# Low parts of split weights from an accumulating transfer, in the planned mixers of a four-layer network

## The chip, the cores and the metric

One core of a Trainium2 chip runs the whole program. The metric is device microseconds of one execution, the median of several runs; less is better.

## The reference

Four layers work on 256 tokens of width 1024, in float32. Each layer is a half-step SwiGLU block, a mixer, and a second half-step SwiGLU block, with root-mean-square norms before and behind each. The mixers are mLSTM (layers 0 and 3), RWKV-7 (layer 1) and retention (layer 2).

```python
for layer in range(DEPTH):
    g = norm_g[layer]
    h = swiglu_ffn(rms_norm(x, g[0]), ffn_w_gu[layer, 0], ffn_w_down[layer, 0])
    x = x + HALF_STEP * rms_norm(h, g[1])
    h = rms_norm(x, g[2])
    kind, j = layer % N_MIXERS, layer // N_MIXERS
    h = mlstm_mixer(...) if kind == 0 else rwkv7_mixer(...) if kind == 1 else retention_mixer(...)
    x = x + rms_norm(h, g[3])
    h = swiglu_ffn(rms_norm(x, g[4]), ffn_w_gu[layer, 1], ffn_w_down[layer, 1])
    x = x + HALF_STEP * rms_norm(h, g[5])
```

mLSTM projects the tokens, convolves q and k, builds input and forget gates, and for each of four heads sums the decayed past: `num = s @ v + inter * (q @ C)`, divided by its denominator, normed by head, gated, and projected back. RWKV-7 has small-rank branches for its decay, its rate and its gate, and a state update for each of 16 heads. For this change only one thing counts: all of it is matrix products with weights of 345 MB in float32, beside the mixers' own small products.

## The kernel before

**Weights.** They come as 345 units of 128 x 2048 float32, 1 MB each. A matmul on float32 weights is made of three on a rounded format (fp32r): every unit is split into a high part, `hi` = the weights rounded, and a low part, `lo` = weights minus `hi`, and `mm3` issues `hi` x high part of the activations, `lo` x high part, `hi` x low part (lines 334 to 336 with the weights standing in the array, 338 to 340 with the weights moving). So nothing of a unit can start until its `hi` is written, and little until its `lo` is.

Four steps bring a unit: `dma()` (L110) puts its load on SyncE's queue into one of `NRAW` = 3 raw buffers; `prep_hi` (L127) lets ScalarE copy, with rounding, from raw to `hi`; `prep_lo` (L135) subtracts `hi` from raw, on VectorE, or on GpSimd if it is handed that engine; and the unit is marked ready. `hi` and `lo` have `NHI` = 5 buffers each. In the FFN blocks and in retention the order of the work is written by hand and a unit is split in two halves of 1024 columns, the subtraction on VectorE. In the two mLSTM layers and in RWKV it is split in quarters of 512 columns.

**The planner.** The bodies of mLSTM and RWKV are written as chains (Python generators): `dense` for the projections, `conv`, `gates`, `attend`, `heads`, `solve`, `finish` and so on, and two `preps` chains that split the weights. Each chain names the engine and the cost in ns of its next piece, or the marks it waits for. `Plan.run` simulates the engines with these costs when the program is built, and takes the piece with the earliest start plus a weight of its chain from the table `PUT_OFF`; VectorE ("ve") and GpSimd ("po") share one resource "port" in it, so that only one of them works at a time there. What it decides is the order of instructions on each engine and nothing else: on the chip every engine takes its own list in that order, and waits at each instruction for what it reads. TensorE can't go past a matmul whose `lo` isn't there.

Of the two `preps` chains one hands its quarters to VectorE (600 ns), the other to GpSimd (1200 ns). They share the same unit: whichever comes first takes the next quarter.

The places that matter are these. In mLSTM, units 36 to 48 in layer 0 (207 to 297 us) and 299 to 311 in layer 3 (1875 to 1985); L925 to L951 make the gates' block of products for a head, L977 and L981 scale it, L993 and L997 are a head's product with its values, L1046 its transposes, L842 the evictions of the projected values, L860 to L871 the convolution. In RWKV, units 115 to 132 (672 to 945 us): L1346 to L1392 form the mixed inputs, L1440 the small-rank products, L1797 to L1881 the inverse for each head pair with the products A16 (L1809), L2020 to L2113 the norm and the last projection, after which L270 to L298 end the layer.

Of the kernel before, what the change touches and what calls it, by code (L numbers as in the profile page):

```python
# [11 lines left out]
F32 = mybir.dt.float32  # L12
# [16 lines left out]
NRAW = 3  # L29
# [5 lines left out]
class Net:  # L35
# [97 lines left out]
    def prep_lo(s, o, src, unit, e=None):  # L133

        (e or s.nc.vector).tensor_tensor(out=o[1], in0=src, in1=o[0].bitcast(F32), op=ALU.subtract)  # L135
        j, h, l, w = unit
        s.split_cols[j] = s.split_cols.get(j, 0) + w
        if s.split_cols[j] < 2048:
            return False
        s.ready[j] = h, l  # L140
        s.dma(j + 1 + NRAW - s.held_raw)
        return True

    def prep_part(s, parts=2, e=None):
        s.prep_lo(*s.prep_hi(parts), e)
# [338 lines left out]
class Stage:  # L484
    HOLD = (0, 0)

    def preps(s, e=None, after=()):
# [4 lines left out]
        while True:  # L492
            yield n.room
            if n.part is None:
                later = [m for m in (("free", n.n_prep + 1 - NHI + n.held_hi), ("raw", n.n_prep)) if m in s.plan.marks]
                if later:
                    yield later
            yield "ac", 520.0
            if not n.room():
                continue  # L500
            o, src, unit = n.prep_hi(4)
            yield ("po", 1200.0) if e else ("ve", 600.0)
            if n.prep_lo(o, src, unit, e):
                s.plan.mark("prep", unit[0])

    def need(s, j):

# [220 lines left out]
class Mlstm(Stage):  # L728
# [1 line left out]


    H, DK, DV = 4, 128, 256
    PUT_OFF = dict(conv=325, gates=300, attend=50, evacs=125, prep=375, prep_po=575, dense=150)
    HEAD = [("v", 0), ("o", 0), ("v", 1)]
    N_AHEAD = 0

# [535 lines left out]
class Rwkv(Stage):  # L1272
# [4 lines left out]

    N_AHEAD = 1
    HOLD = (1, 0)
    PUT_OFF = dict(enter0=500, enter1=450, tail=825, small=150, lora1=275, borrows=250, mix1=50, mix0=200, inv0=50,  # L1280
                   inv1=300, finish=250, norm_in=850, preset=575, evacs=650, w=850, a=875, g=775, norms=175, solve0=350,
                   solve1=250, solve2=225, solve3=325, outputs=375, tr0=150, tr1=675, prep=625, prep_po=450, dense=100,
                   out=775, vec0=300, vec1=175, vec2=600, vec3=425, start0=0, start1=850, start2=425, start3=325,
                   right0=300, right1=0, right2=100, right3=900, rmats0=575, rmats1=425, rmats2=250, rmats3=50, dense2=675)
    ALPHA = math.exp(-0.5)

    def __init__(s, n, gi, d):
# [1057 lines left out]
```

## Time and profile before

| | before |
|---|---|
| median of 3 runs | 2175.19 us (2174.14 to 2177.9) |
| the profiled execution | 2175.98 us, span 2174.2 us |
| mean granted TensorE clock | 0.983 |
| TensorE, VectorE, ScalarE, GpSimd busy | 96%, 69%, 51%, 16% |
| read from HBM | 372.89 MB, 172 GB/s over the span |

The profiled execution is 0.8 us above the median. A busy share is of the whole span. In a window's row the granted clock is a share of full speed, and the DMA share that of 16 DMA engines. "A <- B" in the waits says that A stood idle until B released it.

### The profile page before, as it was taken

What the parts mean: (1) busy time and instruction counts of PE and PEld (TensorE: products, weight loads), DVE (VectorE), ACT (ScalarE), POOL (GpSimd) and SP (SyncE); (2) the same over time, 40 slices, a digit from 0 to 9 for tenths busy, and PEclk for the clock granted to TensorE, in tenths of its full rate; (3) what the DMA queues carried; (4) which work ended last, traced back from release to release, by engine and by line L of the source; (5) the groups of instructions that cost most, each with busy time, mean ns of one, the idle gap of its engine ahead of it and who ended that gap; (6) DMA issues with size and microseconds to landing.
All of it is one profiled execution on the core that took longest, in us unless ns stands there. A gap on an engine that the chain in (4) does not pass through costs nothing.

```text
span 2174.2 us, 38941 instructions
## 1 busy us (share of the span) xinstructions
PE 2091.4 (96%) x16136; PEld 1976.0 (91%) x16136; DVE 1492.2 (69%) x2234; ACT 1112.9 (51%) x1804; POOL 356.2 (16%) x615
## 2 busy tenths in 40 slices
PE   8999989999998999879999999999999999998998
PEld 8999879999997988879999999998999999887997
DVE  6766777667666787677677668556766766757765
ACT  5545655445445754345445445444544554655543
POOL 2001421002000466730001003211000100252000
PEclk9999999999999999889999999999999999999999
DMA  7553245555552320136546555554654555234651
GB/s 278 214 201 136 108 171 211 211 191 195 216 192 98 124 76 31 55 145 251 195 156 244 204 194 194 175 175 146 230 204 169 217 211 194 100 117 191 233 205 68
DMA packets 56226, 376.46 MB, mean 173 GB/s; under 512 B 7144, under 2 KB 8808, under 8 KB 11888
## 3 DMA queue, kind: packets, MB, share of 16 engines
q1 hardware_dynamic: 55472, 372.59, 46.9%
q8 instruction: 127, 2.08, 0.4%
q10 hardware_dynamic: 576, 1.38, 0.2%
q14 instruction: 51, 0.42, 0.1%
HBM read 372.89 MB, written 1.05 MB: 172 GB/s over the span
## 4 chain that ended last, share of the span: by engine, by line
PE 82%; DVE 11%; ACT 3%; issue 2%; POOL 1%; DMA 1%; DVEq 0%; SPq 0%; ACTq 0%; POOLq 0%
PE mm L338 14%; PE mm L340 14%; PE mm L339 14%; PE acc L336 7%; PE acc L334 7%; PE acc L335 7%; PE mm L334 4%; PE mm L335 4%; PE mm L336 4%; DVE lo L135 3%; DVE s L864 1%; ACT hi L127 1%; DVE s L270 1%; DVE x L276 1%; PE acc L1440 1%
## 5 line engine op out<-in xcount | busy, mean ns | idle before, releaser
L135 DVE TENSOR_TENSOR lo<-raw,hi 128x1024 fp32r<-128x1024 f32 (+1 forms) x700 | 810.3, 1200 | 188.6 <-ACT hi L127 186.2
L127 ACT ACTIVATE hi<-raw 128x1024 fp32r<-128x1024 f32 (+1 forms) x766 | 697.7, 964 | 116.5 <-issue 57.0
L338 PE MATMUL mm<-xh,hi 128*128 128x256 f32 x2688 | 743.1, 276 | 0.0
L339 PE MATMUL mm<-xl,hi 128*128 128x256 f32 x2688 | 741.3, 276 | 0.0
L340 PE MATMUL mm<-xh,lo 128*128 128x256 f32 x2688 | 741.2, 276 | 0.0
L339 PEld LDWEIGHTS mm<-xl,hi 128*128 128x128 f32 x2688 | 518.0, 193 | 1.7
L338 PEld LDWEIGHTS mm<-xh,hi 128*128 128x128 f32 x2688 | 518.0, 193 | 1.7
L340 PEld LDWEIGHTS mm<-xh,lo 128*128 128x128 f32 x2688 | 518.1, 193 | 0.0
L336 PE MATMUL acc<-hi,s 128*128 128x512 f32 x864 | 331.3, 383 | 7.4 <-DVE s L1067 6.3
L334 PE MATMUL acc<-hi,s 128*128 128x512 f32 x864 | 333.9, 387 | 4.3 <-ACT s L1063 2.3
L335 PE MATMUL acc<-lo,s 128*128 128x512 f32 x864 | 330.0, 382 | 0.0
L571 ACT ACTIVATE s<-s 128x256 f32<-128x256 f32 x152 | 63.6, 419 | 431.9 <-DVE s L569 431.9
L334 PE MATMUL mm<-hi,xh 128*128 128x256 f32 x960 | 268.8, 280 | 5.3 <-ACT xh L1392 5.3
L335 PE MATMUL mm<-lo,xh 128*128 128x256 f32 x960 | 265.4, 276 | 0.9 <-DVE lo L135 0.9
L336 PE MATMUL mm<-hi,xl 128*128 128x256 f32 x960 | 265.2, 276 | 0.0
L336 PEld LDWEIGHTS acc<-hi,s 128*128 128x128 f32 x864 | 164.9, 191 | 34.1 <-DVE s L1067 7.9
L252 POOL TENSOR_SCALAR rr_v<-ssx 128x1 f32<-128x1 f32 x22 | 5.2, 236 | 1148.7 <-ACT junk L307 1148.6
L334 PEld LDWEIGHTS mm<-hi,xh 128*128 128x128 f32 x960 | 185.5, 193 | 6.8 <-ACT xh L1392 5.6
L334 PEld LDWEIGHTS acc<-hi,s 128*128 128x128 f32 x864 | 165.2, 191 | 26.7 <-ACT s L1063 3.4
L335 PEld LDWEIGHTS mm<-lo,xh 128*128 128x128 f32 x960 | 185.4, 193 | 2.5 <-DVE lo L135 1.3
L336 PEld LDWEIGHTS mm<-hi,xl 128*128 128x128 f32 x960 | 185.4, 193 | 0.2 <-DVE xl L1394 0.2
L335 PEld LDWEIGHTS acc<-lo,s 128*128 128x128 f32 x864 | 165.2, 191 | 21.0
(408 smaller groups left out, 2206.5 us busy)
## 6 DMA issues: line engine op xcount, KB each, us to landing
raw<-in_w SPq DMA_DIRECT2D x345, 1024.0 KB, 4.8
s<-in_g_post SPq DMA_DIRECT2D x12, 512.0 KB, 5.9
x<-in_x ACTq DMA_DIRECT2D x2, 512.0 KB, 6.0
s<-in_rw_l SPq DMA_DIRECT2D x4, 256.0 KB, 6.1
s<-in_rw_ln SPq DMA_DIRECT2D x8, 128.0 KB, 4.2
out<-x SPq DMA_DIRECT2D x3, 256.0 KB, 2.1
s<-in_decay SPq DMA_DIRECT2D x1, 512.0 KB, 6.7
s<-in_rw_zmask SPq DMA_DIRECT2D x1, 320.0 KB
```

The lines of the kernel that those rows point to most:

```text
L127: s.nc.scalar.activation(out=o[0], in_=src, func=AF.Copy)
L135: (e or s.nc.vector).tensor_tensor(out=o[1], in0=src, in1=o[0].bitcast(F32), op=ALU.subtract)
L270: nc.vector.tensor_tensor(out=hg[:, h, :], in0=acc[h], in1=g[:, h * 512:h * 512 + 512], op=ALU.mult)
L276: nc.vector.scalar_tensor_tensor(out=s.x[t][:, c], in0=hg[:, h, :], scalar=r, in1=s.x[t][:, c], op0=ALU.mult, op1=ALU.add)
L334: mm(out, ah, wh, start=first, stop=False)
L335: mm(out, ah, wl, start=False, stop=False)
L336: mm(out, al, wh, start=False, stop=last)
L338: mm(out, wh, ah, start=first, stop=False)
L339: mm(out, wh, al, start=False, stop=False)
L340: mm(out, wl, ah, start=False, stop=last)
L571: nc.scalar.activation(out=sg, in_=gn[:, 0, :], func=AF.Silu)
L864: nc.vector.scalar_tensor_tensor(out=c[:, g, :], in0=x[:, g, j:j + T], scalar=s.cw[:, 4 * g + h, j:j + 1], in1=c[:, g, :], op0=ALU.mult, o ...
```

## The change

The GpSimd chain no longer subtracts. It takes a whole unit; ScalarE copies each quarter to `hi` and then writes `lo` = −`hi` (a copy with scale −1.0); when all four quarters stand, GpSimd issues one transfer that reads the unit again from HBM and adds it into `lo`, `lo` = −`hi` + weights. The planner is told 520 ns of ScalarE for each piece and 1500 ns of GpSimd for the issue, and that the unit is ready 4000 ns behind that, with 2700 ns of the DMA resource. Only one unit can be in part in that chain, so either chain waits for the other where it used to share. The weights `PUT_OFF` of both planned mixers are replaced. The diff, where the last table's rows are cut:

```diff
--- before.py
+++ after.py
@@ -141,6 +141,10 @@
         s.dma(j + 1 + NRAW - s.held_raw)
         return True
 
+    def prep_add(s, j, l):
+
+        s.nc.gpsimd.dma_start(out=l, in_=s.w[j], accum_op=ALU.add)
+
     def prep_part(s, parts=2, e=None):
         s.prep_lo(*s.prep_hi(parts), e)
 
@@ -495,13 +499,39 @@
                 later = [m for m in (("free", n.n_prep + 1 - NHI + n.held_hi), ("raw", n.n_prep)) if m in s.plan.marks]
                 if later:
                     yield later
+            if e and n.part is not None:
+                yield lambda: n.part is None
+                continue
             yield "ac", 520.0
-            if not n.room():
+            if not n.room() or e and n.part is not None:
                 continue
             o, src, unit = n.prep_hi(4)
-            yield ("po", 1200.0) if e else ("ve", 600.0)
-            if n.prep_lo(o, src, unit, e):
+            if e:
+
+                j, h, l, w = unit
+                raw = n.part[0]
+                n.part = None
+                n.n_prep = j + 1
+                yield from s.prep_dma(j, raw, h, l)
+                continue
+            yield "ve", 600.0
+            if n.prep_lo(o, src, unit):
                 s.plan.mark("prep", unit[0])
+
+    def prep_dma(s, j, raw, h, l):
+        n = s.n
+        for q in range(4):
+            c = slice(q * 512, q * 512 + 512)
+            if q:
+                yield "ac", 520.0
+                n.nc.scalar.activation(out=h[:, c], in_=raw[:, c], func=AF.Copy)
+            yield "ac", 520.0
+            n.nc.scalar.activation(out=l[:, c], in_=h.bitcast(F32)[:, c], func=AF.Copy, scale=-1.0)
+        yield "po", 1500.0
+        n.prep_add(j, l)
+        n.ready[j] = h, l
+        n.dma(j + 1 + NRAW - n.held_raw)
+        s.plan.load("prep", j)
 
     def need(s, j):
 
@@ -730,7 +760,7 @@
 
 
     H, DK, DV = 4, 128, 256
-    PUT_OFF = dict(conv=325, gates=300, attend=50, evacs=125, prep=375, prep_po=575, dense=150)
+    PUT_OFF = dict(conv=950, gates=750, attend=375, evacs=925, prep=925, prep_po=975, dense=650)
     HEAD = [("v", 0), ("o", 0), ("v", 1)]
     N_AHEAD = 0
 
@@ -1277,11 +1307,12 @@
 
     N_AHEAD = 1
     HOLD = (1, 0)
-    PUT_OFF = dict(enter0=500, enter1=450, tail=825, small=150, lora1=275, borrows=250, mix1=50, mix0=200, inv0=50,
...
+    PUT_OFF = dict(enter0=350, enter1=675, tail=650, small=325, lora1=975, borrows=1000, mix1=525, mix0=650, inv0=450,
...
     ALPHA = math.exp(-0.5)
 
     def __init__(s, n, gi, d):
```

The planner's lists come out otherwise in the three stages, and only there; TensorE has as many instructions as before. Lines 147 to 495 move by 4 in the changed kernel, later ones by 30, and from L1310 on by 31. By the lists, the subtractions of 512 columns on GpSimd go from 66 (18, 30 and 18) to none, those on VectorE from 22 to 28 in each mLSTM and from 42 to 52 in RWKV; ScalarE gets 44 negations, and GpSimd 11 transfers: units 39, 42 and 44; 123, 125, 127, 130 and 132; 302, 305 and 307.

**Layer 0's mLSTM, around unit 44.** In names like `hi44_3023` the number after `hi` is the unit; `s_249` and the like are small tiles. ScalarE before:

```order
L842 ACT_TABLE_LOAD
L842 ACTIVATE s_249_2991<-mm_240_2909,rs0_98 128x256
L842 ACTIVATE s_249_2991<-mm_240_2909,rs1_99 128x256
L1063 ACTIVATE s_251_3001<-mm_250_2996,ml_g_35_407 128x256 x2
L127 ACTIVATE hi44_3023<-raw44_2800 128x512 x3
L868 ACTIVATE s_241_2922<-s_247_2960 128x2x256
L977 ACT_TABLE_LOAD
L977 ACTIVATE s_256_3068<-mm_254_3044,ml_acol_202_2584 128x256
L977 ACTIVATE s_256_3068<-mm_254_3044,ml_acol_202_2584 128x128
```

and now:

```order
L127 ACTIVATE hi45_2892<-raw45_2819 128x512
L529 ACTIVATE lo44_2884<-hi44_2883 128x512
L527 ACTIVATE hi44_2883<-raw44_2761 128x512
L529 ACTIVATE lo44_2884<-hi44_2883 128x512
L527 ACTIVATE hi44_2883<-raw44_2761 128x512
L872 ACTIVATE s_246_3012<-mm_239_2920,rs0_98 128x256
L872 ACTIVATE s_246_3012<-mm_239_2920,rs1_99 128x256
L529 ACTIVATE lo44_2884<-hi44_2883 128x512
L1093 ACTIVATE s_249_3025<-mm_248_3020,ml_g_35_407 128x256 x2
```

Before, unit 44's quarters are copied once, and the evictions of unit 42's product stand ahead of them (L842). Now three negations (L529) stand ahead of those evictions (L872) and the last one behind.

TensorE there, where head 2's product with its values (L993) stood between units 43 and 44 (`s_259` is that of L842), before:

```order
L334 MATMUL mm_253_3010<-hi43_2871,xh_152_2054 128x256
L335 MATMUL mm_253_3010<-lo43_2872,xh_152_2054 128x256
L336 MATMUL mm_253_3010<-hi43_2871,xl_153_2055 128x256
L993 MATMUL mm_260_3097<-s_259_3088,s_257_3069 128x256 x3
L997 MATMUL mm_255_3045<-ones_91,s_257_3069 128x1 x3
L334 MATMUL mm_261_3107<-hi44_3023,xh_152_2054 128x256
L335 MATMUL mm_261_3107<-lo44_3024,xh_152_2054 128x256
```

and now:

```order
L340 MATMUL mm_258_3100<-hi44_2883,xl_153_2055 128x256
L1023 MATMUL mm_260_3136<-s_259_3113,s_257_3092 128x256 x3
L1027 MATMUL mm_255_3069<-ones_91,s_257_3092 128x1 x3
L338 MATMUL mm_258_3100<-hi44_2883,xh_152_2054 128x256
L339 MATMUL mm_258_3100<-lo44_2884,xh_152_2054 128x256
```

That product now comes behind the first 24 matmuls of unit 44, and it is unit 44's `lo` that the transfer makes.

**RWKV's entry.** TensorE before, behind the last matmul of the FFN (L1351 transposes a tile of 128 tokens, `acc` and `mm` are PSUM tiles):

```order
L336 MATMUL acc_493_5659<-hi114_7152,s_595_7084 128x512
L1351 MATMUL mm_629_7359<-ident_90,s_628_7355 128x128 x4
L1351 MATMUL mm_632_7376<-ident_90,s_628_7355 128x128 x4
L334 MATMUL mm_640_7426<-hi115_7251,xh_606_7297 128x256
L335 MATMUL mm_640_7426<-lo115_7252,xh_606_7297 128x256
L336 MATMUL mm_640_7426<-hi115_7251,xl_607_7298 128x256
```

and now:

```order
L340 MATMUL acc_493_5662<-hi114_7155,s_595_7087 128x512
L1382 MATMUL mm_629_7349<-ident_90,s_628_7346 128x128 x4
L1382 MATMUL mm_630_7362<-ident_90,s_628_7346 128x128 x4
L1471 MATMUL acc_639_7430<-s_608_7285,s_620_7330 128x128
L1471 MATMUL acc_639_7430<-s_610_7287,s_624_7334 128x128
```

Where unit 115 followed, the 32 small-rank products (L1440 before, L1471 now) come first, and unit 115 after them.

**RWKV, around unit 125.** GpSimd before:

```order
L135 TENSOR_TENSOR lo124_8210<-raw124_8115,hi124_8209 128x512 x2
L1756 TENSOR_SCALAR s_689_8042<-s_689_8042,rw_par_487_5650,rw_ka1_546_6419 128x256 x2
L135 TENSOR_TENSOR lo125_8271<-raw125_8193,hi125_8270 128x512
L1809 TENSOR_TENSOR q_661_7809<-q_661_7809,ident_90 128x512 x2
L1758 TENSOR_TENSOR s_673_7958<-s_673_7958,s_689_8042 128x512
L1760 TENSOR_TENSOR gx_663_7811<-s_673_7958,s_706_8139 128x512
L135 TENSOR_TENSOR lo125_8271<-raw125_8193,hi125_8270 128x512
L1766 TENSOR_TENSOR s_673_7958<-s_711_8273,s_673_7958 128x512
```

and now:

```order
L1787 TENSOR_SCALAR s_684_8014<-s_684_8014,rw_par_487_5653,rw_ka1_546_6422 128x256 x2
L1789 TENSOR_TENSOR s_672_7912<-s_672_7912,s_684_8014 128x512
L1791 TENSOR_TENSOR gx_663_7835<-s_672_7912,s_705_8123 128x512
L1797 TENSOR_TENSOR s_672_7912<-s_711_8223,s_672_7912 128x512
L1799 TENSOR_TENSOR s_711_8223<-s_711_8223,s_704_8122 128x512
L1840 TENSOR_TENSOR q_661_7833<-q_661_7833,ident_90 128x512
L146 DMA lo125_8299<-in_w 128x2048
L1745 COPY s_728_8410<-ident_90 8x256
L1840 TENSOR_TENSOR q_661_7833<-q_661_7833,ident_90 128x512
```

The four subtractions between go, and the transfer for unit 125 is issued between the two products A16 (L1809 before, L1840 now). In the order of TensorE 24 matmuls of unit 124 and two groups of four head products stand between the first of these products and unit 125.

More of the change, by code (lines that the diff above doesn't have):

```diff
@@ L1279 @@
     HOLD = (1, 0)
-    PUT_OFF = dict(enter0=500, enter1=450, tail=825, small=150, lora1=275, borrows=250, mix1=50, mix0=200, inv0=50,
[L1281 to L1284, printed above, removed]
+    PUT_OFF = dict(enter0=350, enter1=675, tail=650, small=325, lora1=975, borrows=1000, mix1=525, mix0=650, inv0=450,
+                   inv1=400, finish=575, norm_in=800, preset=1175, evacs=450, w=900, a=575, g=800, norms=125, solve0=150,
+                   solve1=325, solve2=350, solve3=600, outputs=675, tr0=1350, tr1=1675, prep=625, prep_po=825, dense=1075,
+                   out=825, vec0=550, vec1=50, vec2=575, vec3=400, start0=1525, start1=925, start2=75, start3=500,
+                   right0=1150, right1=600, right2=750, right3=500, rmats0=500, rmats1=200, rmats2=525, rmats3=750,
+                   dense2=625)
     ALPHA = math.exp(-0.5)
```

## The prediction

> **What bounds the kernel now.** I read the page's span and engine rows first, then the chain that ended last, the costliest groups and the DMA part, then the stretches in which the planner sets the order.
>
> ```profile
> span 2174.2 us, 38941 instructions
> PE 2091.4 (96%) x16136; PEld 1976.0 (91%) x16136; DVE 1492.2 (69%) x2234; ACT 1112.9 (51%) x1804; POOL 356.2 (16%) x615
> q1 hardware_dynamic: 55472, 372.59, 46.9%
> PE 82%; DVE 11%; ACT 3%; issue 2%; POOL 1%; DMA 1%; DVEq 0%; SPq 0%; ACTq 0%; POOLq 0%
> raw<-in_w SPq DMA_DIRECT2D x345, 1024.0 KB, 4.8
> ```
>
> TensorE is busy for 96% of the span and carries 82% of the chain; VectorE carries 11%. The change removes no TensorE instruction, so all it can win are the 2174.2 − 2091.4 = 82.8 us in which TensorE stands, and stretches at a lower clock. The windows say where those lie: first the mLSTM of layer 0, the RWKV layer and the mLSTM of layer 3, then RWKV's inside and its exit into the next FFN. Columns are us, busy time of each engine, granted clock, DMA share, GB/s.
>
> ```profile
> 207.00:297.00 90.00, 82.34 (x602) 76.46 (x601) 60.48 (x117) 54.85 (x110) 37.43 (x76) 0.94 0.36 134
> 672.00:945.00 273.00, 239.96 (x2302) 217.85 (x2301) 205.02 (x413) 152.22 (x361) 142.00 (x179) 0.94 0.23 84
> 1875.00:1965.00 90.00, 81.78 (x607) 76.12 (x606) 60.65 (x117) 54.65 (x111) 37.45 (x76) 0.96 0.38 135
> 752.00:932.00 180.00, 162.92 (x1713) 147.18 (x1712) 133.60 (x262) 87.60 (x216) 127.26 (x164) 0.94 0.18 63
> 932.00:952.00 20.00, 10.36 (x37) 8.23 (x36) 14.97 (x32) 7.38 (x13) 0.00 (x0) 0.66 0.55 209
> ```
>
> TensorE stands 7.7 us in the first mLSTM, 8.2 in the second and 33.0 in RWKV, of which 17.1 lie inside (752 to 932) and 9.6 at the exit. The rest, about 34 us, lies where the order is written by hand and no unit changes hands. So at most about 49 us are in play, and the kernel outside these stretches I count as unchanged. The waits of TensorE, mLSTM 0 first, RWKV behind:
>
> ```profile
> PE acc L993 <- DVE s L981: 2.7, 2, 1.8
> PE mm L993 <- ACT s L842: 1.8, 1, 1.8
> PE mm L1046 <- DVE s L1025: 0.8, 1, 0.8
> ```
> ```profile
> PE mm L292 <- DVE x L276: 8.3, 1, 8.3
> PE mm L334 <- ACT xh L1392: 5.3, 1, 5.3
> PE acc L1879 <- DVE gx L1869: 2.1, 3, 1.0
> ```
>
> Nowhere does TensorE wait for a low part made by GpSimd; it waits for VectorE and ScalarE. GpSimd matters by what it does to VectorE.
>
> **The subtractions on GpSimd go.** There are 66 of them, 18 + 30 + 18, and these are the rows on them and on VectorE's own, the third and fourth from mLSTM 0 and RWKV:
>
> ```profile
> L135 POOL TENSOR_TENSOR lo<-raw,hi x66: 1263/1286/1871, 209.5 to 1961.3; 128x512 fp32r<-128x512 f32 x66
> L135 DVE TENSOR_TENSOR lo<-raw,hi x43: 657/696/2117, 672.4 to 938.0; 128x512 fp32r<-128x512 f32 x39, 128x1024 fp32r<-128x1024 f32 x4
> L135 DVE TENSOR_TENSOR lo<-raw,hi 128x512 fp32r<-128x512 f32 x21 | 19.2, 916 | 1.8 <-ACT hi L127 1.8
> L135 DVE TENSOR_TENSOR lo<-raw,hi 128x512 fp32r<-128x512 f32 x39 | 39.2, 1010 | 11.7 <-ACT hi L127 9.8 <-issue 1.9
> ```
>
> And at the end of RWKV, first with GpSimd's subtraction beside them, then without:
>
> ```profile
> 917.95 1.73 POOL L135 TENSOR_TENSOR lo<-raw,hi 128x512 fp32r<-128x512 f32 x1
> 918.47 1.24 DVE L2079 TENSOR_SCALAR rw_st<-rw_st 128x4 f32<-128x4 f32 x1
> 919.74 0.65 DVE L206 TENSOR_SCALAR nr_y<-rw_st 128x4 int32<-128x4 int32 x1
> 920.74 0.88 DVE L220 TENSOR_TENSOR nr_u<-nr_y 128x4 f32<-128x4 f32 x1
> 923.03 1.13 DVE L240 TENSOR_SCALAR rw_rs<-nr_y 128x4 f32<-128x4 f32 x1
> 924.20 1.45 DVE L2085 TENSOR_TENSOR s<-s,rw_rs 128x256 f32<-128x256 f32 x1
> 927.99 1.75 DVE L135 TENSOR_TENSOR lo<-raw,hi 128x512 fp32r<-128x512 f32 x1
> 930.98 0.17 DVE L2079 TENSOR_SCALAR rw_st<-rw_st 128x4 f32<-128x4 f32 x1
> 931.19 0.17 DVE L206 TENSOR_SCALAR nr_y<-rw_st 128x4 int32<-128x4 int32 x1
> 931.39 0.16 DVE L220 TENSOR_TENSOR nr_u<-nr_y 128x4 f32<-128x4 f32 x1
> 932.97 0.17 DVE L240 TENSOR_SCALAR rw_rs<-nr_y 128x4 f32<-128x4 f32 x1
> 933.17 0.43 DVE L2085 TENSOR_TENSOR s<-s,rw_rs 128x256 f32<-128x256 f32 x1
> ```
>
> One quarter on VectorE takes 0.70 us in the median, but 1.01 in RWKV's mean and 0.92 in mLSTM's. The timeline shows why: the same instruction on four numbers a partition lasts 1.24 us while GpSimd subtracts and 0.17 twelve microseconds later, when it has stopped. VectorE is held while GpSimd subtracts. On quarters alone that is 39 × (1.01 − 0.70) = 12.1 us in RWKV and 21 × (0.92 − 0.70) = 4.6 in an mLSTM.
>
> The Trainium skill, SBUF — State Buffer, section "Who interferes with whom", has a rule for this: an instruction of VectorE with two SBUF inputs comes through the read interface that GpSimd reads by, and one of the two waits. The rows agree for the subtractions and the products; they go beyond it for the four-number TENSOR_SCALAR. By the rule, GpSimd's products, which stay, hold VectorE as well.
>
> At RWKV's exit these six instructions lie in one chain on VectorE, up to the last projection and the FFN's norm, and no matmul is left to cover it: the first waiter is L292, with 8.3 us. The excess is 1.07 + 0.48 + 0.72 + 0.96 + 1.02 + 1.05 = 5.3 us. GpSimd's products at L2062 to L2077 stay, so I take −4 (bounds −5.3 and 0). Inside RWKV, VectorE is relieved of up to 12.1 us but takes over ten quarters (by the order 52 in place of 42): 10 × 0.70 = 7.0, net −5 of its 205. TensorE there stands 17.1 us, in many pieces of at most 1 us or so that VectorE ends, as the L1879 row has them. I take a third of it, −5.7, as a quarter on VectorE shrinks by a third (bounds: −8.5, half, and +4, since every piece is also a place of the new order). In an mLSTM VectorE takes six quarters more, 4.2 us, for the 4.6 won: nothing, at 60.5 busy of 90.
>
> **The negations on ScalarE.** 44 more copies of 512 elements, 12 + 20 + 12, at a third of the first row's time, 0.55 us: 6.6 us in an mLSTM, 11.1 in RWKV.
>
> ```profile
> 238.33 1.66 ACT L127 ACTIVATE hi<-raw 128x512 fp32r<-128x512 f32 x3
> 275.98 0.84 ACT L842 ACTIVATE s<-mm,rs 128x256 f32<-128x256 f32 x2
> ```
>
> ScalarE is busy for 54.9 of 90 and 152.2 of 273 us, so it has 35 and 121 idle; I cost them at nothing but for the place in the queue, counted with the orders below. If that cover is gone, a later copy for the next unit costs 0.6 us each time.
>
> **The adding transfers.** Eleven of 1 MB, three, five and three, issued by GpSimd. The trace has none, so I bound one. Below: the plain load, 4.8 us, plus one GpSimd quarter of 1.3 us for its issue, 6.1. Above: twice the load and that, 10.9. Between them stands a full second pass: q1's 372.59 MB are 355.3 units of 1.05 MB, and their packets take 46.9% of 2174.2 us, 2.87 us a unit, which gives 9.0. I take half of that pass, 7.5, as nearest to the plain row, the one such row there is. Their traffic is no bound: the DMA share is 0.36 and 0.23.
>
> What counts is whether the transfer lands before TensorE asks. TensorE's rows around a gate block:
>
> ```profile
> 249.16 0.28 PE L335 MATMUL mm<-lo,xh 128*128 128x256 f32 x1
> 249.27 0.28 PE L336 MATMUL mm<-hi,xl 128*128 128x256 f32 x1
> 249.38 0.60 PE L1046 MATMUL mm<-ident,s 128*128 128x128 f32 x4
> 251.25 0.36 PE L338 MATMUL mm<-xh,hi 128*128 128x256 f32 x1
> ```
>
> Dense matmuls start 0.11 us apart, and a group of transposes with the gate block L946 to L951 takes 1.9 us, from 249.38 to 251.25. Unit 44: its last negation stands on ScalarE behind the pair L842 that evicts unit 42's product, so it ends 0.84 + 0.55 = 1.4 us after unit 42 does. TensorE still has 48 matmuls of unit 43 (5.3) and one such group with its block (1.9): 7.2 us, so 5.8 are left. At 7.5 the wait is 1.7, at 6.1 0.3, at 10.9 5.1. Counted alike, unit 39 has 12 us left and unit 42 8.6, so they wait only above that. In RWKV unit 125's transfer is issued right behind the first of the two products A16 (L1809), and ahead of the unit TensorE has 24 matmuls of unit 124 (2.7 us) and two groups of four small head products that wait for that A16, some 2.3 with their wait, an estimate by the block above: 5.0 left, 2.5 of wait at 7.5. Units 123, 127, 130 and 132 have 5 to 8 or more: nothing at 7.5.
>
> The Trainium skill, Collectives: The Full Stack, section "Why ReduceScatter is half of AllGather", speaks against this: an add needs two source reads, and its rate was half of a copy's. By it the full second pass would be due, and the sum would be that of rival 1's transfers, 4.5 us higher; no row here shows it.
>
> **The new orders.** mLSTM, by the waits above: unit 39's twelve matmuls no longer stand ahead of head 0's L993, so its 0.9 grows by their 1.4; at head 1 the scaling L977, which feeds L981, is moved ahead of the convolution's activation L868 on ScalarE, and the 1.8 goes; head 1's transposes L1046 get twelve matmuls of unit 43 ahead of them, −0.8; head 2's L993, 1.8 behind L842, comes after 24 of unit 44 and waits no more; head 3's L993 loses part of its cover as unit 45 is taken earlier, +1.1 by half of those 24. The sum is 1.4 − 1.8 − 0.8 − 1.8 + 1.1 = −1.9. With unit 44's +1.7 an mLSTM gives −0.2, both −0.4 (bounds −3.8 and +6.4, unit 44's wait from none to 5.1). RWKV's entry: 32 small-rank products (L1440) now stand ahead of unit 115, and the mixes on ScalarE and VectorE that feed them pace TensorE where it had dense work; L334 waits 5.3 for L1392 there already. Fewer quarters ahead of the norm speak for less, the pacing for more: +2 (bounds −2 and +6).
>
> **The sum.** mLSTM −0.4, exit −4, inside −5.7, entry +2, unit 125 +2.5: −5.6 on the profiled execution's 2175.98, 2170.4. That execution is 0.8 above the median of the three runs, 2175.19; on that base, which the rivals' times use too, it is 2169.6. I say 2170. What a measurement of this kernel can tell from no change is about 0.2%, 4.4 us.
>
> **The rivals.**
> 1. The gains are eaten by late transfers. At the full second pass, 9.0 us, unit 44 and its twin in layer 3 wait 3.2 each and unit 125 4.0: 1.5 × 3 = 4.5 more than in my sum. Unit 42's 8.6 is passed by 0.4, twice, and if the gain inside RWKV is a half of mine the sum is −5.6 + 4.5 + 0.8 + 2.9 = +2.6, 2177.8. For it: VectorE's net relief is only 5 us of 205. Against: the chain's VectorE rows at the exit.
> 2. Slower: an adding transfer takes 10.9 us, the load twice, or more. Then unit 44 and its twin wait 5.1 each and unit 125 5.9, 3 × 3.4 = 10.2 above my sum; units 42 and 305 lack 2.3 each, 123, 127 and 130, with 5 to 8, some 4 each, +16.6; −5.6 + 10.2 + 16.6 = +21.2, 2196.4. It decides from where the sum passes 4.4, at about 9.5 us. For it: nothing in this trace reads two sources. Against: 4.8 us for a plain load while the queues are idle over half the time.
> 3. Slower by the order: RWKV's entry at +6 and inside at +4, with the exit unchanged since GpSimd's products still hold VectorE: −0.4 + 0 + 4 + 6 + 2.5 = +12.1, 2187.3. For it: 17 of RWKV's 33 idle us lie inside and 5 in the row of L1392.
> 4. The change does less than it says, with VectorE held by GpSimd's other work as before: exit and inside at a quarter, −0.4 − 1 − 1.4 + 2 + 2.5 = +1.7, 2176.9, within 0.2%; counted with rival 1.
>
> **How the numbers follow.** The forecast, a gain of over 4.4 us, 0.48; rivals 1 and 4, 0.27; rival 2, 0.15; rival 3, 0.10. Faster is the first, same the second, slower the last two, 0.25. The likeliest case's own range goes from 2155.6 (mLSTM −1.9 twice, exit −5.3, inside −8.5, entry −2, no wait: −19.6) to 2170.8. The whole one reaches from 2157, with a little of that end left out, to 2187, rival 3's value; rival 2's 2196 is left out.
>
> **What would show it.** No L135 on POOL, VectorE quarters near 0.70 us in both mixers, and the L2079 to L2085 chain at RWKV's exit under 3 us where it took 6 would show the relief; L292's wait stays near 8. The time from GpSimd's issue to landing decides rivals 1 and 2: about 7.5 or less is the forecast; above 9 there is a new TensorE wait on a DMA at units 44, 307 and 125. An idle of over 15 us at 672 to 692 would show rival 3. The forecast is wrong above all if TensorE, which runs in its written order, stands behind one late low part while later units are ready.

## The result and the profile after

The changed kernel takes 2209.46 us (median of 4 runs, 2209.06 to 2212.5) where the kernel before, in the runs beside it, takes 2176.18: a ratio of 1.0159 with a 95% interval of 1.0146 to 1.0171, 33 us slower. I had forecast 2170 and a range of 2157 to 2187. Rival 2 is what happened, and it is worse than I had it.

The page after, on the profiled execution (2209.24 us): span, engines, DMA queues, the chain that ended last, and issues to landing.

```profile
span 2207.5 us, 38892 instructions
PE 2099.7 (95%) x16136; PEld 1982.8 (90%) x16136; DVE 1466.0 (66%) x2256; ACT 1141.9 (52%) x1852; POOL 274.8 (12%) x560
q1 hardware_dynamic: 55472, 372.59, 46.3%
q0 software_dynamic: 1584, 11.54, 2.8%
PE 82%; DVE 8%; ACT 5%; DMA 3%; issue 2%; POOL 0%; DVEq 0%; SPq 0%; ACTq 0%
raw<-in_w SPq DMA_DIRECT2D x345, 1024.0 KB, 4.8
lo<-in_w POOLq DMA_DIRECT2D x11, 1024.0 KB, 9.7
```

DMA has 3% of the chain where it had 1%, VectorE 8% where it had 11%. An adding transfer lands 9.7 us behind its issue in the median. The rows of the eleven, of TensorE's waits, and of VectorE's quarters in mLSTM 0 and RWKV:

```profile
DMA to landing us min/median/max: 8.0/9.7/11.4
PE mm L344 <- DMA lo<-in_w: 18.9, 2, 10.0
PE mm L339 <- DMA lo<-in_w: 9.7, 4, 3.6
L135 DVE TENSOR_TENSOR lo<-raw,hi 128x512 fp32r<-128x512 f32 x28 | 18.9, 682 | 1.8 <-ACT hi L127 1.6
L135 DVE TENSOR_TENSOR lo<-raw,hi 128x512 fp32r<-128x512 f32 x51 | 37.9, 752 | 24.4 <-ACT hi L127 24.0
```

TensorE waits 28.6 us for six of the eleven transfers: two in RWKV (L344) and four in the mLSTM layers (L339). In L342 to L344, before L338 to L340, the weights stand in the array, and in L338 to L340, before L334 to L336, they move; where the kernel before is described, the two are the wrong way round. VectorE's relief is there as told: a quarter takes 0.68 us where it took 0.92, and 0.75 where it took 1.01. It doesn't help while TensorE stands.

The two long waits are at units 123 and 125. ScalarE, GpSimd and TensorE around unit 123, from the timeline:

```profile
754.56 0.63 ACT L529 ACTIVATE lo<-hi 128x512 fp32r<-128x512 f32 x1
755.49 0.95 POOL L146 DMA_DIRECT2D lo<-in_w  x1 [1.60 <-ACT lo L529]
765.60 0.55 PE L344 MATMUL mm<-q,lo 128*128 128x256 f32 x1 [10.02 <-DMA lo<-in_w]
765.95 0.42 PE L342 MATMUL mm<-q,hi 128*128 128x256 f32 x1
```

The last negation ends at 755.2, GpSimd, which waited for it, issues at 755.5, and TensorE arrives at 755.6: 765.60 less the 10.02 that it waits. Next to no time lies between the issue and the need. And when it goes on, its matmuls take 0.42 us where 0.28 is usual, and start 0.21 us apart where 0.11 is usual, until 770.2: the granted clock is 0.50 from 760.0 to there.

That is the second cost. The mean granted clock over the span, of before, after and four kernels told below (no11 without the transfers, memset with GpSimd writing zeros, split4, mix), by their views of cores:

```profile
core 0: 2174.2 us, clock 0.983
core 0: 2207.5 us, clock 0.976
core 0: 2170.7 us, clock 0.981
core 0: 2143.6 us, clock 0.989
core 0: 2201.5 us, clock 0.971
core 0: 2167.6 us, clock 0.982
```

The share not granted is (1 − 0.983) × 2174.2 = 37 us before and (1 − 0.976) × 2207.5 = 53 after. Not all of these 16 us are lost time: at unit 123 the clock goes to half at 760.0, and TensorE stands until 765.6 anyway. What the slow clock can have cost shows in TensorE's busy time, 2099.7 us where it was 2091.4 for the same 16136 matmuls: 8.3 of the 33 us. For the other 25 TensorE stands, 107.8 us in all where it stood 82.8.

By stage, from the last start of the SwiGLU activation (L571, L601 after) in the FFN ahead of a mixer to the first in the one behind it, less the same of before, in us; the other kernels are told below. The last column is the timed median less that of before in the same runs:

| kernel | mLSTM 0 | RWKV | mLSTM 3 | whole |
|---|---|---|---|---|
| after | +0.7 | +23.0 | +9.3 | +33.3 |
| no2 | +3.7 | −0.3 | +8.9 | +12.8 |
| no11 | −2.0 | +0.5 | −1.7 | −2.8 |
| plain | −2.0 | +16.8 | −1.5 | +14.5 |
| sub | +1.6 | +9.5 | +2.5 | +9.8 |
| split4 | −0.9 | +27.3 | +0.9 | +24.7 |
| fix10 | −4.6 | +23.4 | −2.4 | +18.0 |
| qadd | −1.8 | +21.8 | +3.1 | +25.0 |
| dveall | +6.1 | +37.0 | +6.8 | +42.4 |
| memset | −13.2 | −5.5 | −11.9 | −29.9 |
| mslong | −9.2 | −5.3 | −11.2 | −27.5 |
| ms22 | −8.8 | −1.6 | −7.6 | −21.6 |
| noneg | −2.1 | +3.7 | −1.5 | −4.9 |
| ne22 | −2.7 | −0.5 | −1.4 | −4.7 |
| mix | −4.6 | +2.2 | −4.0 | −6.7 |

The two mLSTM layers have the same order, and yet after has +0.7 and +9.3: their transfers landed after 9.2, 9.7 and 8.0 us in the first and after 9.6, 11.3 and 9.3 in the second. A stage's number is good to some 3 us: no2, which changes nothing in the mLSTM layers, has +3.7 and +8.9, and noneg and no11, which differ little, have +3.7 and +0.5 in RWKV. The stages are those of one profiled execution, which lies some 4 us above its kernel's median in sub, split4, ms22 and noneg and 8 above in dveall, so they need not add up to the last column.

### The profile page after: what moved, and what is told of

Its sections match the earlier page's. It is cut to its first block, busy times and chain, and to the rows that moved or that the text cites. A ratio compares the mean times of both kernels' runs of the same rounds, so it can differ in the third digit from the quotient of the medians.

```text
span 2207.5 us, 38892 instructions
## 1 busy us (share of the span) xinstructions
PE 2099.7 (95%) x16136; PEld 1982.8 (90%) x16136; DVE 1466.0 (66%) x2256; ACT 1141.9 (52%) x1852; POOL 274.8 (12%) x560
## 4 chain that ended last, share of the span: by engine, by line
PE 82%; DVE 8%; ACT 5%; DMA 3%; issue 2%; POOL 0%; DVEq 0%; SPq 0%; ACTq 0%
PE mm L342 14%; PE mm L344 14%; PE mm L343 14%; PE acc L340 7%; PE acc L338 7%; PE acc L339 7%; PE mm L339 4%; PE mm L338 4%; PE mm L340 4%; DMA lo<-in_w 3%; DVE lo L135 2%; ACT hi L127 2%; DVE s L274 1%; DVE x L280 1%; PE mm L1990 1%
## 5 line engine op out<-in xcount | busy, mean ns | idle before, releaser
L342 PE MATMUL mm<-xh,hi 128*128 128x256 f32 x2688 | 742.5, 276 | 0.0
L344 PE MATMUL mm<-xh,lo 128*128 128x256 f32 x2688 | 740.8, 276 | 0.0
L127 ACT ACTIVATE hi<-raw 128x1024 fp32r<-128x1024 f32 (+1 forms) x733 | 680.3, 978 | 109.0 <-issue 56.5
L342 PEld LDWEIGHTS mm<-xh,hi 128*128 128x128 f32 x2688 | 517.7, 193 | 1.7
L344 PEld LDWEIGHTS mm<-xh,lo 128*128 128x128 f32 x2688 | 517.6, 193 | 0.0
L340 PE MATMUL acc<-hi,s 128*128 128x512 f32 x864 | 331.8, 384 | 9.1 <-DVE s L1097 8.1
L338 PE MATMUL acc<-hi,s 128*128 128x512 f32 x864 | 334.4, 387 | 5.6 <-ACT s L1093 2.6
L339 PE MATMUL acc<-lo,s 128*128 128x512 f32 x864 | 330.5, 383 | 0.0
L601 ACT ACTIVATE s<-s 128x256 f32<-128x256 f32 x152 | 63.6, 418 | 432.7 <-DVE s L599 432.7
L339 PE MATMUL mm<-lo,xh 128*128 128x256 f32 x960 | 267.5, 279 | 9.7 <-DMA lo<-in_w 9.7
L338 PE MATMUL mm<-hi,xh 128*128 128x256 f32 x960 | 270.6, 282 | 0.0
L340 PE MATMUL mm<-hi,xl 128*128 128x256 f32 x960 | 266.8, 278 | 0.0
L339 PEld LDWEIGHTS mm<-lo,xh 128*128 128x128 f32 x960 | 187.2, 195 | 11.7 <-DMA lo<-in_w 6.3
L340 PEld LDWEIGHTS acc<-hi,s 128*128 128x128 f32 x864 | 165.2, 191 | 35.7 <-DVE s L1097 9.8
L338 PEld LDWEIGHTS acc<-hi,s 128*128 128x128 f32 x864 | 165.5, 192 | 28.7 <-ACT s L1093 3.5
L338 PEld LDWEIGHTS mm<-hi,xh 128*128 128x128 f32 x960 | 187.0, 195 | 1.3 <-issue 1.0
L340 PEld LDWEIGHTS mm<-hi,xl 128*128 128x128 f32 x960 | 187.2, 195 | 0.0
L339 PEld LDWEIGHTS acc<-lo,s 128*128 128x128 f32 x864 | 165.6, 192 | 21.1
L599 DVE TENSOR_TENSOR s<-mm,R 128x512 f32<-128x512 f32 x152 | 104.6, 688 | 83.9 <-PE mm L344 83.9
```

Source lines behind the costliest of these rows:

```text
L127: s.nc.scalar.activation(out=o[0], in_=src, func=AF.Copy)
L338: mm(out, ah, wh, start=first, stop=False)
L339: mm(out, ah, wl, start=False, stop=False)
L340: mm(out, al, wh, start=False, stop=last)
L342: mm(out, wh, ah, start=first, stop=False)
L344: mm(out, wl, ah, start=False, stop=last)
```

## The experiments

Each edit is against the changed kernel unless the text says otherwise, and is shortened.

### Is it the transfers, or the new order?

**no2.** The changed kernel without the transfers of units 123 and 125; the rest stands where it stood.

```diff
-        n.prep_add(j, l)
+        j in (123, 125) or n.prep_add(j, l)
```

> The changed kernel without the transfers of units 123 and 125 (their low parts stay the negated high parts, so two units lack their low parts); every other instruction stands where it stood. Theory A, late landing: TensorE's waits of 10.0 and 8.9 us for these two and the two half-clock stretches of 10.24 us behind them go, and little else: 2180 to 2186. Theory B, the new order and the added work of ScalarE are slow by themselves, and TensorE would have stood there anyway for something else: 2200 or more, with another wait in place of the 18.9 us.

Measured: 2188.11 us, 21 less than after, ratio to before 1.0056 (1.0041 to 1.0071). That is 2 us above theory A's range and far from B's. RWKV comes back by 23.3 us, to −0.3. The two waits are 18.9 of these; the other 4 fit the slow stretches, since TensorE is busy 4.9 us less than in after (2094.8 us). What remains slow are the mLSTM layers, +3.7 and +8.9, with four waits of 10.5 us in both.

**no11.** None of the eleven.

```diff
-        n.prep_add(j, l)
+        pass
```

> The changed kernel without any of the eleven adding transfers (eleven units lack their low parts); the order is the same. Theory A: all 28.6 us of waits for these transfers and the half-clock stretches behind them go, 2170 to 2178, so that order, negations and VectorE's relief together come out at about the kernel before, or below it. Theory B: 2190 or more.

Measured: 2172.55 us, ratio 0.9987 (0.9977 to 0.9996). So the transfers cost 36 us (+33.3 against −2.8), and everything else in the change, VectorE's relief, 44 negations and the new orders, comes out at −2.8. Theory A holds. But 2.8 us is little for relief, and I come back to it.

### What makes a transfer late?

**plain.** The same transfers without the addition.

```diff
-        s.nc.gpsimd.dma_start(out=l, in_=s.w[j], accum_op=ALU.add)
+        s.nc.gpsimd.dma_start(out=l, in_=s.w[j].bitcast(F32R))
```

> The changed kernel with eleven plain transfers of the same units by the same queue at the same places, without the addition (eleven units have the whole weights as low parts). If the second source read makes the transfer slow: landing 5 to 7 us after the issue where it is 9.7 with the addition, TensorE's waits at units 123 and 125 about 6 and 5, at 42, 44, 305 and 307 none: 2186 to 2193. If it is GpSimd's queue and its issue: landing still at 9 to 10 us, 2205 to 2210.

Measured: 2189.84 us, ratio 1.0074 (1.0054 to 1.0094): the first case, with waits of 5.8 and 6.2 us at units 123 and 125. Queue, landing and waits:

```profile
q0 software_dynamic: 1584, 11.54, 1.5%
lo<-in_w POOLq DMA_DIRECT2D x11, 1024.0 KB, 6.8
PE mm L344 <- DMA lo<-in_w: 12.0, 2, 6.2
```

The addition takes the DMA engines 2.8% of 2207.5 us for 11 units, 5.6 us each, where the plain copy takes 1.5% of 2187.4, 3.0 us. The time to landing goes from 6.8 to 9.7. So the order of sizes is: 4.8 us for a plain load on SyncE's queue, 2.0 more for the plain copy on GpSimd's, 2.9 more for the addition. The plain copy also writes a tile of the rounded format, which the load doesn't, so the 2.0 need not be the queue's alone. The Trainium skill, Collectives: The Full Stack, section "Why ReduceScatter is half of AllGather", says of a collective's reduce that its add needs two source reads; the two transfers here agree, with 1.9 times the engines' time. And yet plain loses 17 us in RWKV: at units 123 and 125 it lands after 7.4 and 7.7 us, so even a transfer of the 7.5 us of my sum comes too late there.

**sub.** GpSimd's four subtractions at the place of each transfer, so a unit is ready 5.2 us later than there.

```diff
-        n.prep_add(j, l)
+        for each quarter c: n.nc.gpsimd.tensor_tensor(out=l[:, c], in0=raw[:, c], in1=h[:, c], op=subtract)
```

> The changed kernel with GpSimd's four subtractions of 512 columns at the place of each transfer, in the new order; 5.2 us a unit. Theory A: waits at units 123 and 125 of about 5 and 4 us, none at 42, 44, 305 and 307, and VectorE held again as before the change for up to 10 us in each mLSTM and 16 in RWKV, of which a part shows: 2185 to 2200, faster than with the transfers although VectorE loses its relief. Theory B (the order is what is slow): 2205 or more.

Measured: 2185.06 us, ratio 1.0044 (1.0029 to 1.0059): as forecast, but not by the waits forecast. TensorE's waits for GpSimd's low parts are 0.8 us:

```profile
PE mm L344 <- POOL lo L531: 0.8, 3, 0.3
```

A unit's quarters come one by one, where the transfer sets one mark for the whole unit: at unit 123 the four end 1.2 us apart, and TensorE waits 0.2, 0.3 and 0.3 us and goes on with each. So an adding transfer at the same places is 24 us worse than the subtractions it replaces, with all that these do to VectorE.

**split4.** Each transfer in four, each behind its own negation.

```diff
+            n.nc.scalar.activation(out=l[:, c], ..., scale=-1.0); n.nc.gpsimd.dma_start(out=l[:, c], in_=n.w[j][:, c], accum_op=ALU.add)
-        n.prep_add(j, l)
```

> The changed kernel with each adding transfer cut into four of 512 columns, each issued as soon as its own quarter is negated; order of all other work unchanged. If the time is that of moving the bytes twice behind the last negation: the last quarter lands 3 to 6 us after its issue, TensorE's 28.6 us of waits fall to 8 to 15: 2188 to 2198. If it is a fixed delay of such a transfer, or four issues of 0.9 us in a row on GpSimd take it back: waits of 25 us or more, 2203 to 2212.

Measured: 2199.69 us, ratio 1.0115 (1.01 to 1.013), between the two forecasts, and by other means than either.

```profile
lo<-in_w POOLq DMA_DIRECT2D x44, 256.0 KB, 8.3
PE mm L344 <- DMA lo<-in_w: 5.2, 2, 3.0
PE mm L339 <- DMA lo<-in_w: 2.4, 4, 1.7
POOL lo L529 <- ACT lo L529: 50.6, 10, 17.9
```

A quarter takes 8.3 us to land, little less than a unit, but TensorE's waits fall to 7.6 us. The mLSTM layers are back at −0.9 and +0.9. RWKV isn't (+27.3): the issues stand earlier in GpSimd's list and wait there for ScalarE, and GpSimd's products behind them are late, as a wait of TensorE of 3.6 us for L1799 shows that the changed kernel doesn't have. The windows around RWKV, of no11 first and of split4 behind, show how its time comes about (engines in the order TensorE, its weight loads, VectorE, ScalarE, GpSimd; then clock, DMA share, GB/s):

```profile
645.00:980.00 335.00, 302.16 (x2693) 274.96 (x2693) 228.61 (x485) 189.97 (x426) 110.99 (x169) 0.93 0.26 91
646.00:1008.00 362.00, 317.68 (x2698) 288.84 (x2698) 234.53 (x485) 190.36 (x426) 123.92 (x189) 0.89 0.32 99
```

TensorE stands 44.3 us in place of 32.8, 11.5 more, and is busy 317.68 in place of 302.16, 15.5 more, with the same work at a granted clock of 0.89 in place of 0.93: together the 27 us. The larger part is the slow clock.

**fix10.** Why was there no time between issue and need? In `prep_dma` the unit is put into `n.ready` when the transfer is issued, and `need()` asks for the unit's mark only if it isn't in that list. So a chain that asks for a unit after its issue doesn't wait for the mark, 4000 ns or more behind, that `load` sets; its matmuls may be placed right behind the issue, and at units 123 and 125 they were. (The change's description says that the planner holds the unit back for these 4000 ns; it does so only where a chain asked before the issue.) fix10 asks for the mark wherever there is one, and sets it 9.7 us behind the issue.

```diff
-        if j not in n.ready:
+        if j not in n.ready or ("prep", j) in s.plan.marks:
             yield [("prep", j)]
...
-        s.plan.load("prep", j)
+        s.plan.marks["prep", j] = s.plan.end + 9700.0
```

> The changed kernel where the planner waits for the unit's mark before it places its matmuls, and the mark stands 9.7 us after the issue as measured; in the changed kernel the unit counts as ready at its issue, as the list of ready units is filled there and need() then skips the mark. The plan is made anew with the same weights. Theory: the wait comes from matmuls placed as if the transfer took no time; with the true time TensorE's waits for transfers fall from 28.6 to under 6 us, 2172 to 2188. Rival: nothing else can be placed there, so TensorE stands for something else or the unit still comes too soon: 2198 or more.

Measured: 2193.05 us, ratio 1.0077 (1.0062 to 1.0092). The first half of the theory holds, the waits for transfers go from 28.6 to 5.2 us; the time lies between the theory's and the rival's, since RWKV stays at +23.4. These are all of its waits for transfers, and the first of its waits in RWKV:

```profile
PE mm L339 <- DMA lo<-in_w: 2.8, 3, 1.9
PE acc L339 <- DMA lo<-in_w: 1.7, 1, 1.7
PE mm L344 <- DMA lo<-in_w: 0.7, 1, 0.7
...
PE acc L340 <- DVE s L2157: 7.9, 2, 6.9
PE mm L350 <- DVE gx L1782: 7.5, 1, 7.5
PE mm L296 <- DVE x L280: 6.3, 1, 6.3
PE mm L1981 <- DVE s L1977: 6.2, 3, 4.7
```

The delay is turned into waits for VectorE: of these rows after has L296 with 6.1 and L1981 with 2.5, and the other two not at all. My reading is that with the dense matmuls placed later less is left to cover RWKV's chains of small products, and that the weights which order them, being those of the other plan, don't fit; no run shows this. In the mLSTM layers, though, the true landing helps: −4.6 and −2.4.

**qadd.** The old order, with each of GpSimd's 66 quarters negated by ScalarE and added by a transfer of 256 KB at its place.

```diff
+        o[1] of GpSimd's quarters: nc.scalar.activation(out=o[1], in_=o[0], func=Copy, scale=-1.0)
+        nc.gpsimd.dma_start(out=o[1], in_=s.w[j][:, columns], accum_op=ALU.add)
```

> The kernel before in its own order, where each of the 66 quarters that GpSimd subtracted is negated by ScalarE and added by a transfer of 256 KB that GpSimd issues at the same place. VectorE's relief as in memset (2145), plus 66 copies on ScalarE and 66 issues. If a quarter lands some 4 to 5 us behind its issue and TensorE takes it later than that: 2148 to 2162. If it comes late as the units did: waits of TensorE for transfers of 15 us or more with their half-clock stretches, 2180 or more.

Measured: 2201.11 us, ratio 1.012 (1.0103 to 1.0137). The second case: 21.9 us of waits for transfers, fifteen of them, though a quarter lands after 5.3 us.

```profile
PE mm L340 <- DMA lo<-in_w: 17.3, 11, 4.4
PE acc L335 <- DMA lo<-in_w: 3.2, 2, 2.0
PE mm L335 <- DMA lo<-in_w: 1.4, 2, 0.7
```

### What is VectorE's relief worth, and where did it go?

**memset.** The kernel before, in its own order, where GpSimd writes zeros and reads nothing.

```diff
-        (e or s.nc.vector).tensor_tensor(out=o[1], in0=src, in1=o[0].bitcast(F32), op=ALU.subtract)
+        e.memset(o[1], 0.0) if e else s.nc.vector.tensor_tensor(...)
```

> The kernel before, in its own order, with GpSimd writing zeros where it subtracted (66 quarters lack their low parts): GpSimd reads no SBUF there, so VectorE isn't held by it, and nothing else moves. It prices the relief by itself. If my terms of relief (exit -4, inside RWKV -5.7, mLSTM 0) hold and the new order ate them: 2163 to 2168. If TensorE's path has other waits behind those: 2171 to 2176.

Measured: 2145.08 us, ratio 0.9861 (0.9846 to 0.9876): 30 us less, more than twice the larger of the two forecasts. Most of it is in the mLSTM layers, where I had priced the relief at nothing. TensorE's waits in the first mLSTM, of memset first and of no11 behind:

```profile
PE acc L993 <- DVE s L981: 1.5, 2, 0.8
PE acc L334 <- ACT s L1063: 1.1, 2, 0.6
PE acc L947 <- ACT s L929: 0.9, 1, 0.9
PE mm L993 <- ACT s L842: 0.6, 1, 0.6
PE acc L336 <- DVE s L1067: 0.4, 2, 0.2
```
```profile
PE acc L340 <- DVE s L1097: 4.1, 2, 3.9
PE acc L1023 <- DVE s L1011: 3.3, 1, 3.3
PE acc L338 <- ACT s L1093: 1.3, 2, 0.7
```

In memset no wait is over 0.9 us, and the granted clock of this stretch is 0.98 where before has 0.92; over the whole span it is 0.989, 24 us not granted where before lost 37. The longest of the waits that are gone is this one of before:

```profile
PE acc L336 <- DVE s L1067: 3.2, 2, 3.0
```

It ends at 300 us and, in layer 3, at 1969. The windows of the prediction ended at 297 and 1965, so its list of waits lacks it; in no11 it is still there, as L340 and L1097.

**mslong.** memset with two and a half writes for one, so that GpSimd is busy as long as its subtraction was.

```diff
-        e.memset(o[1], 0.0)
+        [e.memset(x, 0.0) for x in (o[1], o[1], o[1][:, :256])]
```

> The kernel memset with two and a half writes in place of one, about 1.3 us of GpSimd for each quarter, as long as its subtraction was, and still no read of SBUF. If it is GpSimd's read that held VectorE: 2145 to 2152. If it is that GpSimd was free sooner, for its own work on the path: 2165 to 2176.

Measured: 2148.35 us, ratio 0.9876 (0.9861 to 0.989), so 27 of the 30 us stay. The engines of memset first and of mslong behind, to be held against VectorE's 1492.2 us and GpSimd's 356.2 in before:

```profile
PE 2079.1 (97%) x16136; PEld 1966.9 (92%) x16136; DVE 1448.7 (68%) x2234; ACT 1111.9 (52%) x1804; POOL 294.3 (14%) x615
PE 2079.0 (97%) x16136; PEld 1966.5 (92%) x16136; DVE 1449.8 (67%) x2234; ACT 1113.0 (52%) x1804; POOL 350.6 (16%) x747
```

With the same 2234 instructions VectorE is busy 43 us less, whether GpSimd writes for 33 us or for 89. It is GpSimd's reading that holds VectorE, not GpSimd's time: the Trainium skill, SBUF — State Buffer, section "Who interferes with whom", says that a two-input instruction of VectorE contends with a GpSimd instruction that reads SBUF and not with one that only writes it, and this pair of runs agrees. One thing stays open: the zeros don't wait for ScalarE's `hi` as the subtractions did, so GpSimd also comes earlier to its own work; no run tells what that gives of the 30 us.

**noneg.** no11's order without the 44 negations too; GpSimd writes zeros in the place of each transfer.

```diff
-            n.nc.scalar.activation(out=l[:, c], in_=h.bitcast(F32)[:, c], func=AF.Copy, scale=-1.0)
-        n.prep_add(j, l)
+        n.nc.gpsimd.memset(l, 0.0)
```

> The changed kernel without the eleven transfers and without the 44 negations (GpSimd writes zeros into the unit where the transfer was issued; eleven units lack their low parts); order of all else as changed. Against no11 (2172.6) it takes away only ScalarE's added work. If the negations are what keeps the relief of 30 us from showing: 2145 to 2158. If it is the new order with VectorE's 22 more quarters: 2167 to 2174.

Measured: 2171.29 us, ratio 0.9977 (0.9965 to 0.9989), against no11's 2172.55: the negations cost nothing that can be told, as predicted.

**ms22 and ne22.** The new plan gives VectorE 22 quarters more. ms22 adds as many to memset's old order, ne22 takes as many (21 by the trace) out of noneg's new one.

```diff
ms22 -        e.memset(o[1], 0.0) if e else subtract on VectorE
ms22 +        e.memset(o[1], 0.0) if e and (count of e) % 3 else subtract on VectorE
ne22 -        subtract on VectorE
ne22 +        nc.gpsimd.memset(o[1], 0.0) if (count of quarters) % 5 == 0 else subtract on VectorE
```

> The kernel memset (old order, GpSimd writing zeros, 2145) with every third of its 66 zeroings done as a subtraction by VectorE at the same place, so 22 more quarters on VectorE, as many as the change adds there; 44 quarters lack their low parts. If VectorE's added quarters (22 x 0.70 = 15 us of its time) eat the relief: 2160 to 2172. If the new order does: 2146 to 2154.

> The mirror of ms22: the kernel noneg (new order, no transfers, no negations, 2171) with every fifth of VectorE's quarters, some 22, zeroed by GpSimd in place of the subtraction; these lack their low parts too. If VectorE's added quarters eat the relief: 2148 to 2158. If the new order does: 2165 to 2172.

Measured: ms22 2154.21 us, ratio 0.9899 (0.9882 to 0.9915); ne22 2171.09, ratio 0.9984 (0.9972 to 0.9996). Both lie with the second case, ms22 at its edge: the added quarters cost 9 us in the old order and nothing that can be told in the new one. With the same quarters on VectorE, no transfer and no negation, the new order (noneg) is 17 us behind the old one (ms22). How the 30 us of relief divide depends on what is taken first: some 9 for VectorE's added share and then 17 for the order, or, from memset to ne22 to noneg, 26 for the order and then nothing for the share. Either way the order is the larger part. I can point at two places of that order in mLSTM, the rows of no11 above: L1023, head 0's product, has lost unit 39's matmuls ahead of it and waits 3.3 us where it waits 0.7 in memset (1.0 in before), and L340 waits 3.9 for L1097 where it waits 0.2 (3.0 in before). For RWKV I have only the sums; which of its many moves cost it stays open.

**dveall.** VectorE makes all low parts, planned anew with the old weights.

```diff
-        chains: prep=preps[0], prep_po=preps[1]
+        chains: prep=preps[0]
```

> The kernel before without GpSimd's chain: VectorE makes every low part, planned anew with the old weights. VectorE takes over 66 quarters at 0.70 us, 46 us in three stages, and is no longer held, about 38 us by the rows of before. If it has the room: 2168 to 2178, as good as with GpSimd's help. If low parts come late (VectorE in RWKV is at 75%): 2182 or more, with waits of TensorE for VectorE's lo.

Measured: 2217.43 us, ratio 1.0188 (1.0171 to 1.0205), the slowest of all. The time is that of the second forecast, but not by its sign: TensorE's waits for VectorE's low parts are 3.4 us in all, and the longest are for other work of VectorE:

```profile
PE mm L2104 <- DVE s L2096: 12.0, 1, 12.0
PE acc L993 <- DVE s L981: 10.4, 2, 5.2
PE acc L335 <- DVE lo L135: 1.9, 2, 1.0
```

VectorE's busy time is 1488.3 us, no more than before's 1492.2, so its added share alone doesn't explain this; the plan, with weights made for two chains, is the suspect, and no run shows it.

**mix.** Transfers in the mLSTM layers alone, with fix10's planner there, and RWKV as it was before the change.

```diff
+    ADD = True      # Mlstm: transfers, and need() waits for the mark; Rwkv: ADD = False
+    RWKV's PUT_OFF and its GpSimd subtractions as before
```

> Transfers in the two mLSTM layers alone, with the planner waiting for their true landing (as fix10), and RWKV as in the kernel before. In fix10 the mLSTM layers took 4.6 and 2.4 us less than before and RWKV 23.4 more, so if stages add up: 2166 to 2171, faster than before by about 0.3%. If an mLSTM's gain was only given by what came ahead of it: 2174 or more.

Measured: 2169.41 us (2166.12 to 2172.68, 7 runs), ratio 0.9969 (0.9956 to 0.9982): faster than both kernels, by 0.3% than before. The mLSTM layers give −4.6 and −4.0, with 2.9 us of waits for transfers left:

```profile
PE mm L339 <- DMA lo<-in_w: 2.9, 3, 1.5
```

## Why the prediction was wrong

The sum was −5.6, of which −11.5 without any wait for a transfer and +5.9 for three waits. Measured are −2.8 without the transfers (no11) and 36 for them. So 30 of the 39 us that are missing lie in the waits, and 9 in gains that didn't come.

- **The adding transfer, 7.5 us: mis-sized.** It is 9.7 (8.0 to 11.4). I had written down 9.0 for a full second pass and gone below it to the middle, with the one plain row as the nearest. The addition alone is 2.9 us, which is the full second pass; the plain copy from GpSimd's queue takes 2.0 more than the load, where I had 1.3.
- **The time left in the mLSTM layers: right.** Unit 44 had 5.8 us by my count and had 5.7 (275.9 − 2.3 − 267.9), and so had its twin, unit 307; unit 42 had 8.6 by my count and 8.8, and waited 1.1 at 9.7 us and, in layer 3 as unit 305, 2.7 at 11.3. Here the waits are wrong by the landing alone.
- **The time left in RWKV: the step that failed.** I had 5.0 us at unit 125, with 2.5 of wait, and 5 to 8 at 123, with none; it was 1.6 and 0.1, and TensorE waited 8.9 and 10.0. I counted matmuls from the transfer's place in GpSimd's list, as if it were issued when GpSimd comes to it. But the issue waits for the last of seven copies on ScalarE (2.85 us at 125, 1.60 at 123), and these stand behind evictions that follow TensorE closely; at 123 they ended as TensorE came to the unit. no2 gives the price of the two: 21 us. With about the landing that I assumed, plain still loses 17 us in RWKV. I had also taken the planner's 4000 ns at its word, which it doesn't wait for at these units.
- **The slow clock: not in the sum.** No term of the sum and no rival's price has it. By TensorE's busy time it is up to 8.3 of the 33 us.
- **mLSTM's order without the waits, −1.9: right as a sum**, −2.0 and −1.7 in no11, and mostly in its parts: the waits at head 1, at the transposes and at head 2 are gone, head 3's is 0.7, and only head 0's went to 3.3 where I had 2.3. But as an account of what relief is worth there it is wrong, since memset gives −13.2 and −11.9 in the old order. "Nothing, at 60.5 busy of 90" read a share of busy time where single waits on VectorE decide, with the slow clock beside them; the longest of these, L336 for L1067, lay behind the end of my windows.
- **RWKV's relief, −4 at the exit and −5.7 inside: not seen.** no11 has +0.5 for the whole layer where the sum without unit 125's wait was −7.7; memset has −5.5. At the exit L296 waits 6.6 us in no11 where it waited 8.3, so some 2 came. The first chain from L2079 to L2085, 7.2 us before, takes 5.9 in after and 3.8 in no11, not under 3: in after a four-number instruction of it, L2110, still takes 2.71 us beside GpSimd's products, and 0.17 without.
- **The entry, +2: not seen.** TensorE stands 4.1 of the first 20 us there, where it stood 6.7, and 6.9 of the first 80, where it stood 7.6.
- **The negations at nothing: right** (noneg against no11).
- **The rivals.** Rival 2, at 0.15, had the mechanism and, among its places, the six at which TensorE waited; the landing, 9.7 us, lies between rival 1's 9.0 and its 10.9. Its price, 2196, lacked the clock, had units 123 and 125 at 4 and 5.9 us, and had waits at 127 and 130, where there were none. That it came nearest is in part luck.

## What to carry to other kernels

A transfer that takes an engine's place is late by its landing, not by its engine time, and an engine that runs in order stands for all of it: count how long before the need it is issued on the slowest of the engines that it waits for, and see that the planner's readiness really is what its users ask for. Price a long TensorE wait with the slow clock beside it; here that came to about a quarter as much again (36 us for 28.6 of waits, and 23.3 for 18.9 in RWKV). And before a change is made that relieves an engine, measure the relief alone, with an instruction at the same place that doesn't do the harm: here it showed 30 us to be had, of which the new order kept 3 to 5 even without its transfers.

## What the runs showed of the hardware

- In the median a transfer of 1 MB lands after 4.8 us plain from SyncE's queue, 6.8 plain from GpSimd's, 9.7 adding from GpSimd's; of 256 KB adding, 8.3 when four follow one another (split4) and 5.3 when they are spread (qadd).
- With zeros written where GpSimd subtracted two SBUF tiles, the kernel takes 30 us less; with zeros written for as long as the subtractions took, 27 less. VectorE's busy time falls by 43 us in both.
- The half clock: in after, from 200 us on, each TensorE wait of 2.5 to 10 us has a stretch of 3.4 to 10.2 us at half the clock that begins within the wait or at most 0.5 us behind it. split4 and no11 differ in RWKV by 15.5 us of TensorE's busy time for the same work, more than by its standing, 11.5.
